# The feed-forward input projection as seven half-size products instead of eight (a two-layer decoder in one core)

## The chip, the cores and the metric

The kernel runs on one core of one Trainium2 chip. The metric is the device time of one execution in microseconds (us), the median of several runs.

## What is computed

Two decoder layers over 512 tokens of width 1024, all in float32. Each layer has a mixer of four branches, a cross-attention to 256 memory tokens, and a SwiGLU feed-forward part, each added to the residual stream `x`. The change touches the feed-forward part alone:

```python
def swiglu(h, w_in, w_out):
    a, b = jnp.split(h @ w_in, 2, axis=-1)
    return (jax.nn.silu(a) * b) @ w_out
...
x = x + swiglu(rmsnorm(x, norm_ffn_g[l]), w_ffn_in[l], w_ffn_out[l])
```

`w_in` is 1024 x 5632 (2 x 2816), `w_out` is 2816 x 1024.

## The kernel before

**Numbers in two pieces.** TensorE multiplies numbers of about 12 significant bits (type fp32r) at full rate. So every float32 operand is split into a rounded part `hi` and the rest `lo`, and a product is three matmuls: hi x hi, hi x lo, lo x hi (`mm3`, line 268). ScalarE makes `hi` by a copy, and VectorE or GpSimd makes `lo` by a subtraction with two inputs.

**The weight stream.** All weights lie in HBM in the order in which they are used, as blocks of 128 x 128, eight blocks (512 KB) to a chunk. `load` (line 227) has SyncE fetch a chunk. `prep` (line 240) makes its `hi` on ScalarE (line 245) and its `lo` (line 248) on GpSimd for three chunks out of five, on VectorE for the other two. `advance` prepares chunks up to three ahead of the one in use; there are four tiles for `hi` and four for `lo`, so the preparation of a chunk waits until TensorE has done with the chunk four before it.

**The order of work.** The program is written out as one Python run; each engine has one queue and works through it in that order. `fm` (line 274) makes products with features on the partitions: outputs are 128 columns of the weights by 512 tokens, one PSUM bank each, summed over the 128-row pieces k of the features. With `outer=True` four columns are summed side by side, so the first input piece serves four products before the second is needed. With `norm`, the statistics of the RMS norm are taken behind those products (`norm_stat`, line 384), the scale `rb` is broadcast by a matmul 18 matmuls later (`norm_bcast`, line 406), and only then are the four banks read out.

**The feed-forward part** (`ffn`, line 1093). Columns of `a` and `b` alternate, 44 in all, 8 pieces k each. `ev` reads an `a` bank (line 1101, times `rb`/2), takes its tanh on ScalarE (1102), forms (1 + tanh) x a (1106), reads the `b` bank (1108), multiplies (1109), and splits the result into `hi` and `lo` at once (lines 343 and 344). All 22 hidden pieces stay on chip in both parts. Then `w_ffn_out`: four output columns side by side over the 22 pieces, then the other four one after another. Each output column goes through `finish_x` (line 356): the bank is added to `x` on VectorE (361), ScalarE scales it (364) and VectorE makes the rest (365) for the next norm's input, ScalarE squares it (369, 372) and VectorE adds up the squares (376). In the last layer lines 364 and 365 are left out and ScalarE scales by the last gain (1132).

On chip there are 59 tiles of 128 x 512 (`unit`) and four tiles of 128 x 4 x 512 (`quad`).

Of the kernel before, what the change touches and what calls it, by code (L numbers as in the profile page):

```python
# [40 lines left out]
PREP = 3  # L41
LOAD = 5
# [15 lines left out]
class Prog:  # L58
    def __init__(self, tc, io):
# [3 lines left out]
        self.raw, self.wt = {}, {}  # L63
        self.nu, self.nq, self.vid = NU, NQ, 0
# [14 lines left out]
    def unit(self, n=1, r=False):  # L79
        """n tiles of [128, 512]; r: for products, of 12 significant bits"""  # L80
# [89 lines left out]
    def turn(self, key, n):  # L170
        """waits for the n-th turn at key"""
# [14 lines left out]
    def go(self, it):  # L186
        """one stage of an item; it yields how many beats its next stage should wait"""
# [39 lines left out]
    def load(self, n):  # L227
        while self.loaded < min(n, NCH):
            i = self.loaded
            r = self.wraw.tile([128, CHB * 128], F32, tag="raw", name="raw")  # L230
            self.nc.sync.dma_start(out=r, in_=self.io["wall"][i])
            self.raw[i] = r
            self.loaded += 1

    def advance(self, ci):
        while self.prepped < min(ci + PREP + 1, NCH):
            self.load(max(ci + LOAD, self.prepped) + 1)
            self.prep()

    def prep(self):  # L240
        nc = self.nc
        i = self.prepped
        r = self.raw.pop(i)
        h = self.whi.tile([128, CHB * 128], F32R, tag="hi", name="hi")
        nc.scalar.activation(out=h, in_=r, func=AF.Copy)  # L245
        lo = self.wlo.tile([128, CHB * 128], F32R, tag="lo", name="lo")
        eng = nc.gpsimd if i > 16 and i % 5 in self.pool_lo else nc.vector
        eng.tensor_tensor(out=lo, in0=r, in1=h.bitcast(F32), op=OP.subtract)  # L248
        self.wt[i] = (h, lo)
        self.prepped += 1  # L250

    def w(self, name, l, k, c0, n=1):
# [1198 lines left out]
```

## Time and profile before

| | before |
|---|---|
| time, median of 3 runs | 2343.83 us (2340.56 to 2344.4) |
| span of the profiled execution, first to last instruction | 2340.9 us |
| TensorE (PE) busy | 2285.5 us, 98% |
| weight loads (PEld) busy | 1835.9 us, 78% |
| VectorE (DVE) busy | 1170.2 us, 50% |
| ScalarE (ACT) busy | 820.9 us, 35% |
| GpSimd (POOL) busy | 656.2 us, 28% |
| mean granted TensorE clock | 0.993 of full speed |

The profile shows one execution. Its page gives the span and no other time of that execution; the span stands 2.9 us below the median of the runs. Busy times add up what the instructions of an engine took; matmuls overlap each other, so TensorE's pace is read from the starts of its matmuls, not from its busy share.

### The profile page before, as it was taken

What the parts mean: (1) busy time and instruction counts of PE and PEld (TensorE: products, weight loads), DVE (VectorE), ACT (ScalarE), POOL (GpSimd) and SP (SyncE); (2) the same over time, 40 slices, a digit from 0 to 9 for tenths busy, and PEclk for the clock granted to TensorE, in tenths of its full rate; (3) what the DMA queues carried; (4) which work ended last, traced back from release to release, by engine and by line L of the source; (5) the groups of instructions that cost most, each with busy time, mean ns of one, the idle gap of its engine ahead of it and who ended that gap; (6) DMA issues with size and microseconds to landing.
All of it is one profiled execution on the core that took longest, in us unless ns stands there. A gap on an engine that the chain in (4) does not pass through costs nothing. (4 is left out here: it accounts for less than half of the span.)

```text
span 2340.9 us, 27338 instructions
## 1 busy us (share of the span) xinstructions
PE 2285.5 (98%) x10714; PEld 1835.9 (78%) x10714; DVE 1170.2 (50%) x2186; ACT 820.9 (35%) x1395; POOL 656.2 (28%) x327
## 2 busy tenths in 40 slices
PE   8999999999999999999999999999999999999997
PEld 6777777777888788888877777777878877888886
DVE  6755443545846554431347563355475655543321
ACT  5323433343234432222323244334423443322231
POOL 2463222213222122222237422222322222222221
PEclk9999999999999999999999999999999999999998
DMA  6122222223234223333322222222223432332331
GB/s 227 51 81 73 78 76 73 81 72 95 78 99 144 72 90 108 99 92 107 122 88 80 67 79 73 73 81 76 92 68 99 138 105 81 90 99 90 100 98 54
DMA packets 61473, 213.70 MB, mean 91 GB/s; under 512 B 7072, under 2 KB 7456, under 8 KB 61088
## 3 DMA queue, kind: packets, MB, share of 16 engines
q1 hardware_dynamic: 60624, 210.18, 28.7%
q8 instruction: 84, 1.38, 0.2%
q10 hardware_dynamic: 576, 1.05, 0.1%
q0 software_dynamic: 144, 0.73, 0.1%
q14 instruction: 45, 0.37, 0.0%
HBM read 207.73 MB, written 4.19 MB: 91 GB/s over the span
## 5 line engine op out<-in xcount | busy, mean ns | idle before, releaser
L266 PE MATMUL ps<-u,hi 128*128 128x512 f32 x4160 | 1301.9, 394 | 1.3 <-ACT u L343 0.7
L248 POOL TENSOR_TENSOR lo<-raw,hi 128x1024 fp32r<-128x1024 f32 x213 | 519.0, 2438 | 1567.8 <-ACT hi L245 1505.3
L266 PEld LDWEIGHTS ps<-u,hi 128*128 128x128 f32 x4160 | 772.6, 188 | 173.8 <-issue 12.9
L266 PE MATMUL ps<-u,lo 128*128 128x512 f32 x2080 | 812.3, 391 | 1.7 <-POOL lo L248 1.7
L245 ACT ACTIVATE hi<-raw 128x1024 fp32r<-128x1024 f32 x372 | 388.8, 1051 | 329.9 <-PE ps L266 220.1
L266 PEld LDWEIGHTS ps<-u,lo 128*128 128x128 f32 x2080 | 391.0, 188 | 85.3 <-POOL lo L248 2.4
L248 DVE TENSOR_TENSOR lo<-raw,hi 128x1024 fp32r<-128x1024 f32 x159 | 209.5, 1320 | 352.2 <-ACT hi L245 351.9
L266 PE MATMUL ps<-hi,u 128*128 128x512 f32 x896 | 289.9, 405 | 11.6 <-ACT hi L245 11.6
L266 PE MATMUL ps<-q,hi 128*128 128x512 f32 x768 | 240.8, 395 | 0.0
L266 PEld LDWEIGHTS ps<-hi,u 128*128 128x128 f32 x896 | 166.1, 192 | 56.0 <-ACT hi L245 12.9
L266 PE MATMUL ps<-lo,u 128*128 128x512 f32 x448 | 178.2, 398 | 6.7 <-POOL lo L248 5.6
L266 PE MATMUL ps<-u 128*64 128x128 f32 (+6 forms) x1208 | 171.0, 338 | 4.3 <-DVE u L418 2.1
L266 PEld LDWEIGHTS ps<-q,hi 128*128 128x128 f32 x768 | 141.3, 188 | 34.0 <-issue 5.2
L266 PEld LDWEIGHTS ps<-u 128*128 128x128 f32 (+2 forms) x1208 | 117.1, 172 | 47.5 <-issue 27.9
L266 PE MATMUL ps<-q,lo 128*128 128x512 f32 x384 | 149.8, 390 | 0.0
L921 ACT ACTIVATE u<-u 128x512 f32<-128x512 f32 x64 | 40.4, 631 | 210.9 <-DVE u L920 210.6
L266 PEld LDWEIGHTS ps<-lo,u 128*128 128x128 f32 x448 | 85.7, 191 | 28.3 <-POOL lo L248 6.9
L920 DVE TENSOR_TENSOR u<-ps,u 128x512 f32<-128x512 f32 x64 | 44.0, 688 | 121.8 <-PE ps L266 121.8
L266 PEld LDWEIGHTS ps<-q,lo 128*128 128x128 f32 x384 | 72.1, 188 | 15.5
L1108 DVE TENSOR_TENSOR u<-ps,u 128x512 f32<-128x512 f32 x44 | 30.4, 692 | 86.7 <-PE ps L266 85.9
L347 PE MATMUL ps<-gcst,u 128*128 128x128 f32 x416 | 65.9, 274 | 5.9 <-DVE u L684 2.8
L347 PEld LDWEIGHTS ps<-gcst,u 128*128 128x128 f32 x416 | 51.2, 140 | 23.0 <-DVE u L684 4.1
(209 smaller groups left out, 1657.2 us busy)
## 6 DMA issues: line engine op xcount, KB each, us to landing
raw<-wall SPq DMA_DIRECT2D x372, 512.0 KB, 3.5
q<-memt SPq DMA_DIRECT2D x6, 512.0 KB, 6.4
q<-xt SPq DMA_DIRECT2D x2, 1024.0 KB, 7.6
u<-rot SPq DMA_DIRECT2D x8, 256.0 KB, 4.1
u<-xt SPq DMA_DIRECT2D x8, 256.0 KB, 6.0
xd<-u SPq DMA_DIRECT2D x8, 256.0 KB, 2.0
u<-xd SPq DMA_DIRECT2D x8, 256.0 KB, 5.0
out<-u SPq DMA_DIRECT2D x4, 256.0 KB, 2.7
```

Source lines behind the costliest of these rows:

```text
L245: nc.scalar.activation(out=h, in_=r, func=AF.Copy)
L248: eng.tensor_tensor(out=lo, in0=r, in1=h.bitcast(F32), op=OP.subtract)
L266: self.nc.tensor.matmul(out, lhsT=a, rhs=b, start=start, stop=stop)
L347: self.nc.tensor.transpose(out, src, self.ident)
L920: nc.vector.tensor_tensor(out=self.U(u), in0=ps, in1=self.U(self.rb), op=OP.mult)
L921: nc.scalar.activation(out=self.U(u), in_=self.U(u), func=AF.Tanh, scale=0.5)
L1108: nc.vector.tensor_tensor(out=self.U(t), in0=ps, in1=self.U(self.rb), op=OP.mult)
```

## The change

Of the 22 pairs of `a` and `b` columns the first three are made as before. For the other 19 the kernel takes one pair of weight columns (two column blocks) by the two halves of the features (4 pieces k each) by the two halves of the tokens (256 each) as a 2 x 2 product of blocks, and makes it by the scheme of Strassen and Winograd: seven block products of 4 k x 3 matmuls with 256 columns (84 in all) stand where 48 matmuls with 512 columns stood.

This needs sums on both sides. On the weight side a pair is two chunks in one `quad`; `prep_halves` makes it ready in four granules: part 0 takes two sums on VectorE (one instruction of 1024 elements per partition, one of 512) and a `lo` of 512, part 1 a third sum of 512 and a `lo` of 1024 on VectorE, parts 2 and 3 each a `lo` of 1024 on GpSimd. On the input side `operands` builds, once per layer and for each of four k, seven operands of 256 tokens from `x`: the norm is multiplied in (two instructions of 512), four sums, seven `hi` on ScalarE, four `lo` on VectorE and three on GpSimd. It is queued as stages behind the first four columns, and `finish("S")` has all of it in the queues before the first of the seven products.

On the output side ScalarE copies the bank of the first running sum out three times, and VectorE forms the four output quarters by four instructions of 256 columns out of PSUM; the gate then works on float32 tiles. The hidden pieces are no longer split when they are made: `split(k)` does it in the output projection, three pieces ahead of TensorE, once in each of three groups of output columns (4, 2, 2). `x` is overwritten by `operands`; it is written to HBM after the cross-attention and read back before the output projection.

```diff
-PREP = 3
-LOAD = 5
+FLY = 4
+RAWS = 3
+FF_PLAIN = 3
+OPS = ("A11", "A12", "A22", "S1", "S2", "S3", "S4")
...
+                q = self.quad()
+                for i in range(2):
+                    self.nc.sync.dma_start(out=self.Q(q)[:, 2 * i:2 * i + 2],
+                                           in_=self.io["wall"][c + i].rearrange("p (a b) -> p a b", a=2))
...
+    def advance(self, g):
+        while self.prepped < len(self.gran) and (self.prepped <= g or self.fly < FLY):
+            assert self.fly < FLY
+            self.load(4)
             self.prep()
+        self.load(4)
...
+    def prep_halves(self, c, part, h, lo):
+        nc, v = self.nc, self.nc.vector
+        B = self.Q(self.raw[c])
+        if part == 0:
+            self.sums = self.quad()
+        S = self.Q(self.sums) if part < 3 else None
+        n = 1 if part == 0 else 2
+        src = (B[:, 0:1], S[:, 0:2] if S is not None else None, S[:, 2:4] if S is not None else None, B[:, 2:4])[part]
+        h3, lo3 = (t.rearrange("p (a b) -> p a b", a=2)[:, :n] for t in (h, lo))
+        if part == 0:
+            v.tensor_tensor(out=S[:, 0:4:3], in0=B[:, 1:3], in1=B[:, 0:2], op=OP.subtract)
+            v.tensor_tensor(out=S[:, 1], in0=S[:, 3], in1=B[:, 0], op=OP.add)
+        nc.scalar.activation(out=h3, in_=src, func=AF.Copy)
+        if part == 1:
+            v.tensor_tensor(out=S[:, 2], in0=S[:, 1], in1=B[:, 3], op=OP.subtract)
+        eng = nc.gpsimd if part >= 2 else v
+        eng.tensor_tensor(out=lo3, in0=src, in1=h3.bitcast(F32), op=OP.subtract)
...
+    def operands(self, g):
+        nc, v = self.nc, self.nc.vector
+        H = T // 2
+        self.ops = []
+        for k in range(KD // 2):
+            a, b = self.x + k, self.x + k + KD // 2
+            for d in (k, k + KD // 2):
+                x = self.U(self.x + d)
+                v.scalar_tensor_tensor(out=x, in0=x, scalar=g[:, d:d + 1], in1=self.U(self.rb), op0=OP.mult, op1=OP.mult)
+            yield 1
+            A11, A21, A12, A22 = (self.U(u)[:, h * H:h * H + H] for u in (a, b) for h in range(2))
+            self.ops.append([self.unit(r=True) for _ in OPS])
+            s = self.unit(2)
+            S1, S2, S3, S4 = (self.U(u)[:, h * H:h * H + H] for u in (s, s + 1) for h in range(2))
+            v.tensor_tensor(out=S1, in0=A21, in1=A22, op=OP.add)
+            v.tensor_tensor(out=S2, in0=S1, in1=A11, op=OP.subtract)
+            v.tensor_tensor(out=S3, in0=A11, in1=A21, op=OP.subtract)
+            v.tensor_tensor(out=S4, in0=A12, in1=S2, op=OP.subtract)
+            yield 1
+            for i, src in enumerate((A11, A12, A22, S1, S2, S3, S4)):
+                u = self.ops[k][i]
+                hi = self.UR(u)[:, :H]
+                nc.scalar.activation(out=hi, in_=src, func=AF.Copy)
+                eng = nc.gpsimd if i in (0, 2, 5) else v
+                eng.tensor_tensor(out=self.UR(u)[:, H:], in0=src, in1=hi.bitcast(F32), op=OP.subtract)
...
+    def product(self, bank, op, w, o, first):
+        H = T // 2
+        i = OPS.index(op)
+        out = self.P(bank)[:, :H]
+        K = len(self.ops)
+        for k in range(K):
+            u = self.UR(self.ops[k][i])
+            s = slice((o * 4 + k) * 128, (o * 4 + k) * 128 + 128)
+            hi, lo = w[0][:, s], w[1][:, s]
+            mm = lambda a, b, start, stop: self.nc.tensor.matmul(out, lhsT=a, rhs=b, start=start, stop=stop,
+                                                                 skip_group_check=not first)
+            mm(hi, u[:, :H], first and k == 0, False)
+            mm(hi, u[:, H:], False, False)
+            mm(lo, u[:, :H], False, k == K - 1)
...
+            nc.scalar.activation(out=s1, in_=half(r1), func=AF.Copy)
+            self.advance(g[1])
+            r5 = self.bank()
+            self.product(r5, "S1", self.wt[g[1]], 0, True)
+            self.product(r1, "S2", self.wt[g[1]], 1, False)
+            nc.scalar.activation(out=s2, in_=half(r1), func=AF.Copy)
+            self.advance(g[2])
+            r3 = self.bank()
+            self.product(r3, "A22", self.wt[g[2]], 0, True)
+            self.product(r1, "S3", self.wt[g[2]], 1, False)
+            nc.scalar.activation(out=s3, in_=half(r1), func=AF.Copy)
+            self.advance(g[3])
+            v.tensor_tensor(out=o2[:, right], in0=half(r5), in1=s3, op=OP.add)
+            v.tensor_tensor(out=o1[:, right], in0=s3, in1=half(r3), op=OP.subtract)
+            r4 = self.bank()
+            self.product(r4, "A12", self.wt[g[3]], 1, True)
+            if j + 1 < len(pairs):
+                enter(j + 1)
+            v.tensor_tensor(out=o1[:, left], in0=half(r4), in1=s1, op=OP.add)
+            self.product(r5, "S4", self.wt[g[3]], 0, False)
+            v.tensor_tensor(out=o2[:, left], in0=half(r5), in1=s2, op=OP.add)
+            after(j)
...
+        def gate(a, b):
+            t = self.unit()
+            nc.scalar.activation(out=self.U(t), in_=self.U(a), func=AF.Tanh, scale=0.5)
+            nc.vector.scalar_tensor_tensor(out=self.U(a), in0=self.U(t), scalar=1.0, in1=self.U(a), op0=OP.add,
+                                           op1=OP.mult)
+            self.release(t)
+            nc.vector.tensor_tensor(out=self.U(a), in0=self.U(a), in1=self.U(b), op=OP.mult)
...
+        cols = [(j // 2) * 128 + (j % 2) * HID for j in range(2 * FF_PLAIN)]
+        self.fm("w_ffn_in", l, cols[:4], self.h(), ev, outer=True,
+                norm=lambda: self.add("S", self.operands(gf)))
         self.fm("w_ffn_in", l, cols[4:], self.h(), lambda j, ps: ev(j + 4, ps))
-        self.release(self.rbh)
+        self.finish("S")
...
+        self.load_x(self.xf)
...
+        def split(k):
+            hi, lo = self.unit(r=True), self.unit(r=True)
+            nc.scalar.activation(out=self.UR(hi), in_=self.U(hd[k]), func=AF.Copy, scale=0.5)
+            nc.vector.scalar_tensor_tensor(out=self.UR(lo), in0=self.U(hd[k]), scalar=0.5, in1=self.U(hi),
+                                           op0=OP.mult, op1=OP.subtract)
+            return hi, lo
+        d0, ready = 0, {}
+        groups = (4, 2, 2)
+        order = [(i, k) for i in range(len(groups)) for k in range(KH)]
+        ahead = iter(order)
+        def more(n):
+            while len(ready) < n and (nxt := next(ahead, None)):
+                ready[nxt] = split(nxt[1])
+        for i, n in enumerate(groups):
+            bs = [self.bank() for _ in range(n)]
+            for k in range(KH):
+                more(3)
+                hi, lo = ready[i, k]
+                for j in range(n):
+                    self.mm3(self.P(bs[j]), self.w("w_ffn_out", l, k, (d0 + j) * 128), (self.UR(hi), self.UR(lo)),
+                             k == 0, k == KH - 1)
+                del ready[i, k]
+                self.release(hi)
+                self.release(lo)
+                if i == len(groups) - 1:
+                    self.release(hd[k])
+            for j, b in enumerate(bs):
+                fin(d0 + j, self.P(b))
+            d0 += n
...
+        def fin(d, ps):
+            self.finish_x(d, ps, gf)
+            nc.sync.dma_start(out=self.xf[d], in_=self.U(self.x + d))
+        self.fm("w_xo", l, c4(0), os_, fin, outer=True, need=heads)
+        self.fm("w_xo", l, c4(512), os_, lambda j, ps: fin(4 + j, ps))
```

VectorE's queue behind the norm of layer 0's feed-forward part, before (lines as above):

```order
L1101 TENSOR_TENSOR u<-ps,u 128x512
L1106 SCALAR_TENSOR_TENSOR u<-u 128x512
L1108 TENSOR_TENSOR u<-ps,u 128x512
L1109 TENSOR_TENSOR u<-u 128x512
L344 TENSOR_TENSOR q<-u,q 128x512
```

And now: L1303 reads a bank, L1294 and L1297 are the gate, L1181 multiplies the norm into `x`, L1187 to L1190 are the four sums, L1197 the `lo` parts (this group of L1181 to L1197 stands there four times, all ahead of the first product):

```order
L1303 TENSOR_TENSOR u<-ps,u 128x512 x2
L1294 SCALAR_TENSOR_TENSOR u<-u 128x512
L1297 TENSOR_TENSOR u<-u 128x512
L1303 TENSOR_TENSOR u<-ps,u 128x512 x2
L1294 SCALAR_TENSOR_TENSOR u<-u 128x512
L1297 TENSOR_TENSOR u<-u 128x512
L1181 SCALAR_TENSOR_TENSOR u<-u,vec 128x512 x2
L1303 TENSOR_TENSOR u<-ps,u 128x512
L1187 TENSOR_TENSOR u<-u 128x256
L1188 TENSOR_TENSOR u<-u 128x256
L1189 TENSOR_TENSOR u<-u 128x256
L1190 TENSOR_TENSOR u<-u 128x256
L1197 TENSOR_TENSOR u<-u 128x256 x4
```

Where VectorE had only reads of banks, gates and splits, 40 instructions of the operands now stand between the gates and the first pair.

VectorE's queue for one pair of the 19, now. L311 and L312 (the two sums), L317 (`lo`, part 0), L315 (third sum) and L317 (`lo`, part 1) prepare the next pair's weights; L1268, L1269, L1275 and L1279 form the four quarters of this pair; L1294 and L1297 are its gate:

```order
L311 TENSOR_TENSOR q<-q 128x2x512
L312 TENSOR_TENSOR q<-q 128x512
L317 TENSOR_TENSOR lo<-q,hi 128x512
L315 TENSOR_TENSOR q<-q 128x512
L317 TENSOR_TENSOR lo<-q,hi 128x1024
L1268 TENSOR_TENSOR u<-ps,u 128x256
L1269 TENSOR_TENSOR u<-u,ps 128x256
L1275 TENSOR_TENSOR u<-ps,u 128x256
L1279 TENSOR_TENSOR u<-ps,u 128x256
L1294 SCALAR_TENSOR_TENSOR u<-u 128x512
L1297 TENSOR_TENSOR u<-u 128x512
```

Before, a pair had the five rows of the first fence and, for two chunks in five, one `lo` of 1024. The seventh product adds to the bank that L1268 reads, so it waits for L1268, and L1268 stands behind the weights of the next pair.

VectorE's queue in the output projection of layer 0, where the first four output columns are done, before:

```order
L361 TENSOR_TENSOR u<-ps,u 128x512
L365 SCALAR_TENSOR_TENSOR u<-u,vec 128x512
L376 TENSOR_TENSOR u<-u 128x512
L248 TENSOR_TENSOR lo<-raw,hi 128x1024 x2
L361 TENSOR_TENSOR u<-ps,u 128x512
```

And now (L439, L443 and L454 are what L361, L365 and L376 were; L1341 is the `lo` of a hidden piece, L293 that of a chunk):

```order
L439 TENSOR_TENSOR u<-ps,u 128x512
L443 SCALAR_TENSOR_TENSOR u<-u,vec 128x512
L454 TENSOR_TENSOR u<-u 128x512
L439 TENSOR_TENSOR u<-ps,u 128x512
L443 SCALAR_TENSOR_TENSOR u<-u,vec 128x512
L454 TENSOR_TENSOR u<-u 128x512
L1341 SCALAR_TENSOR_TENSOR u<-u 128x512
L293 TENSOR_TENSOR lo<-raw,hi 128x1024
L1341 SCALAR_TENSOR_TENSOR u<-u 128x512 x8
```

Ahead of the four `finish_x` stand 24 rows of L1341, for the 22 pieces of the first group and two of the second; the third piece of the second group stands behind them.

## Rows read from the trace of the kernel before

**Rows 1.** The page: the span, and each engine's busy time.

```profile
span 2340.9 us, 27338 instructions
...
PE 2285.5 (98%) x10714; PEld 1835.9 (78%) x10714; DVE 1170.2 (50%) x2186; ACT 820.9 (35%) x1395; POOL 656.2 (28%) x327
```

**Rows 2.** The chain that ended last, longest piece: start us, us, engine and line.

```profile
1988.10 334.39 PE ps L266 x1472
```

**Rows 3.** TensorE's timeline, plain columns, layer 0: start us, us, form, count.

```profile
1041.04 0.39 PE L266 MATMUL ps<-u,lo 128*128 128x512 f32 x1
...
1041.72 0.39 PE L266 MATMUL ps<-u,lo 128*128 128x512 f32 x1
```

**Rows 4.** TensorE's timeline: eight transposes of 128 columns in a run.

```profile
1656.16 1.04 PE L347 MATMUL ps<-gcst,u 128*128 128x128 f32 x8
```

**Rows 5.** Lines 248 and 1109: duration ns min/median/max.

```profile
L248 DVE TENSOR_TENSOR lo<-raw,hi x159: 1207/1225/3229, 9.4 to 2290.8; 128x1024 fp32r<-128x1024 f32 x159
...
L248 POOL TENSOR_TENSOR lo<-raw,hi x213: 2354/2397/2930, 100.3 to 2301.7; 128x1024 fp32r<-128x1024 f32 x107
...
L1109 DVE TENSOR_TENSOR u<-u x44: 691/692/2414, 853.8 to 2203.6; 128x512 f32<-128x512 f32 x44
```

**Rows 6.** Timeline of GpSimd and VectorE together, feed-forward input, layer 0.

```profile
875.34 5.22 POOL L248 TENSOR_TENSOR lo<-raw,hi 128x1024 fp32r<-128x1024 f32 x2 [4.90 <-ACT hi L245]
...
876.34 1.96 DVE L1106 SCALAR_TENSOR_TENSOR u<-u 128x512 f32<-128x512 f32 x1 [0.70 <-ACT u L1102]
...
879.13 1.98 DVE L1109 TENSOR_TENSOR u<-u 128x512 f32<-128x512 f32 x1
```

**Rows 7.** The same view where both engines work on 256 columns.

```profile
556.06 0.92 POOL L603 TENSOR_TENSOR u<-u 128x256 f32<-128x256 f32 x1
556.30 0.96 DVE L604 TENSOR_TENSOR u<-u 128x256 f32<-128x256 f32 x1
556.94 0.92 POOL L605 TENSOR_TENSOR u<-u 128x256 f32<-128x256 f32 x1
```

**Rows 8.** Groups of VectorE by form: busy us, mean ns; 256 columns out of PSUM.

```profile
L635 DVE TENSOR_TENSOR u<-ps,gcst 128x256 f32<-128x256 f32 x16 | 6.0, 415 | 2.9 <-PE ps L266 2.9
```

**Rows 9.** The page: ScalarE's `hi` of a chunk; DMA issues, KB, us to landing.

```profile
L245 ACT ACTIVATE hi<-raw 128x1024 fp32r<-128x1024 f32 x372 | 388.8, 1051 | 329.9 <-PE ps L266 220.1
...
u<-xd SPq DMA_DIRECT2D x8, 256.0 KB, 5.0
```

**Rows 10.** Timeline behind the first four columns of the feed-forward part, layer 0.

```profile
842.25 1.84 PE L266 MATMUL ps<-gcst,u 128*128 128x1 f32 x16
...
849.68 0.60 ACT L409 ACTIVATE u<-ps 128x512 f32<-128x512 f32 x1 [6.41 <-PE ps L266]
850.31 0.63 ACT L1123 ACTIVATE u<-u 128x512 f32<-128x512 f32 x1
```

**Rows 11.** Timeline, `finish_x` of four columns: first and last row, layers 0 and 1.

```profile
1121.03 0.69 DVE L361 TENSOR_TENSOR u<-ps,u 128x512 f32<-128x512 f32 x1 [12.14 <-PE ps L266]
...
1130.82 0.68 DVE L376 TENSOR_TENSOR u<-u 128x512 f32<-128x512 f32 x1
...
2260.63 1.37 DVE L361 TENSOR_TENSOR u<-ps,u 128x512 f32<-128x512 f32 x2 [6.70 <-PE ps L266]
...
2267.28 0.69 DVE L376 TENSOR_TENSOR u<-u 128x512 f32<-128x512 f32 x1 [0.70 <-ACT u L372]
```

**Rows 12.** TensorE's timeline: the first matmul after an idle stretch.

```profile
143.20 0.62 PE L266 MATMUL ps<-u,stri 128*128 128x512 f32 x1 [3.79 <-POOL u L795]
```

**Rows 13.** Busy time by stretch: us, five engines, PEclk, DMA share, GB/s.

```profile
143.43:146.84 3.41, 3.03 (x7) 2.15 (x7) 1.18 (x2) 0.60 (x1) 3.41 (x4) 0.50 0.00 0
```

**Rows 14.** Timeline of the last column's `finish_x`.

```profile
2322.51 0.69 DVE L361 TENSOR_TENSOR u<-ps,u 128x512 f32<-128x512 f32 x1 [12.88 <-PE ps L266]
2323.24 0.63 ACT L372 ACTIVATE u<-u 128x512 f32<-128x512 f32 x1 [13.57 <-DVE u L361]
```

More of the change, by code (lines that the diff above doesn't have):

```diff
@@ L224, in beat, with plan @@
             self.step()
-    def load(self, n):
[L228 to L237, printed above, removed]
+    def plan(self):
+        plain = lambda n: ["n"] * (n // CHB)
+        head = plain(64)
+        layer = lambda: plain(928 + 16 * FF_PLAIN) + ["s"] * FF_HALVES + plain(8 * KH)
+        kinds = head + layer() + layer()
+        gran, c = [], 0
+        for kind in kinds:
+            if kind == "n":
+                gran.append(("n", c, 0))
+                c += 1
+            else:
+                gran += [("s", c, i) for i in range(4)]
+                c += 2
+        assert c == NCH, (c, NCH)
+        return gran, {(c, i): n for n, (_, c, i) in enumerate(gran)}
@@ new lines, in load @@
+    def load(self, n):
+        for _ in range(n):
+            if self.loaded == len(self.gran):
+                return
+            kind, c, _ = self.gran[self.loaded]
+            if kind == "n":
+                if self.raws == RAWS:
+                    return
+                r = self.wraw.tile([128, CHB * 128], F32, tag="raw", name="raw")
+                self.nc.sync.dma_start(out=r, in_=self.io["wall"][c])
+                self.raw[c] = r
+                self.raws += 1
+                self.loaded += 1
+            else:
+                if self.pairs == 2:
+                    return
+                q = self.quad()
+                for i in range(2):
+                    self.nc.sync.dma_start(out=self.Q(q)[:, 2 * i:2 * i + 2],
+                                           in_=self.io["wall"][c + i].rearrange("p (a b) -> p a b", a=2))
+                self.raw[c] = q
+                self.pairs += 1
+                self.loaded += 4
@@ L246, in prep @@
         lo = self.wlo.tile([128, CHB * 128], F32R, tag="lo", name="lo")
[L247 to L250 removed]
+        if kind == "n":
+            r = self.raw.pop(c)
+            self.raws -= 1
+            nc.scalar.activation(out=h, in_=r, func=AF.Copy)
+            eng = nc.gpsimd if c > 16 and c % 5 in self.pool_lo else nc.vector
+            eng.tensor_tensor(out=lo, in0=r, in1=h.bitcast(F32), op=OP.subtract)
+        else:
+            self.prep_halves(c, part, h, lo)
@@ new lines, in prep @@
+        self.wt[self.prepped] = (h, lo)
+        self.prepped += 1
+        self.fly += 1
+    def prep_halves(self, c, part, h, lo):
[15 more added lines that the diff above has]
+        eng.tensor_tensor(out=lo3, in0=src, in1=h3.bitcast(F32), op=OP.subtract)
+        if part == 2:
+            self.release(self.sums, 4)
+        if part == 3:
+            self.release(self.raw.pop(c), 4)
+            self.pairs -= 1
@@ L252, in w, with done @@
+    def done(self, g):
+        if self.wt.pop(g, None):
+            self.fly -= 1
     def w(self, name, l, k, c0, n=1):
@@ L1120, in ffn @@
-        cols = [(j // 2) * 128 + (j % 2) * HID for j in range(2 * KH)]
-        def half():
-            self.rbh = self.unit()
-            nc.scalar.activation(out=self.U(self.rbh), in_=self.U(self.rb), func=AF.Copy, scale=0.5)
-        self.fm("w_ffn_in", l, cols[:4], self.h(), ev, outer=True, norm=half)
-        self.fm("w_ffn_in", l, cols[4:], self.h(), lambda j, ps: ev(j + 4, ps))
-        self.release(self.rbh)
+                ua[j] = u
+            else:
+                gate(ua.pop(j - 1), u)
```

118 lines of the change are left out of this document (76 added, 42 removed).

## The prediction

> **What bounds the kernel now.** I read the page first: TensorE is busy for 98% of the span, VectorE for 50%, ScalarE for 35%, GpSimd for 28% [rows 1]. The chain of waits says the same of the part that changes: from 1988 us to the end of layer 1's feed-forward part it is one piece of 334 us on TensorE [rows 2]. So there every matmul saved is time saved, as long as no other engine takes over. TensorE's timeline gives its pace: three matmuls of 512 columns from 1041.04 to 1041.72 [rows 3], 0.227 us each. A pair of `a` and `b` columns is 48 of them, 10.9 us.
>
> The averages hide who would take over. The timeline of GpSimd and VectorE does not [rows 6]. GpSimd starts a `lo` at 875.34; alone it takes 2.40 us [rows 5], so it is done at 877.74. VectorE starts a gate instruction with two inputs in SBUF at 876.34; it should take 0.69 us and ends at 878.30, 0.56 us after GpSimd. GpSimd's second `lo` is done at 875.34 + 5.22 = 880.56, which is 2.26 us after VectorE's end; VectorE's next one ends at 881.11, 0.55 us later. So the two take turns, with some 0.14 us of each hidden: in turns, 512 columns cost VectorE 0.55 us and 1024 columns cost GpSimd 2.26 us. On 256 columns the turns are 0.28 us (from 556.98 to 557.26) and 0.60 us (to 557.86) [rows 7]. The maxima of lines 248 and 1109, 3.2 and 2.4 us against 1.2 and 0.69 [rows 5], are such waits. With GpSimd rarely needed this cost nothing; the change needs both engines much more.
>
> **The products.** A pair becomes 84 matmuls of 256 columns, and no row shows one of this type. From below: each loads its own 128 x 128 weights, and eight transposes in a run, bound by such loads, take (1.04 - 0.27)/7 = 0.11 us each [rows 4], 0.27 being the last one's own duration. From above: 512 columns at 2.4 GHz are 0.213 us, so a matmul carries 0.0135 us beyond its columns; if that is paid whole for half the columns, 0.107 + 0.0135 = 0.120 us. If it shrinks with them it is half of 0.227, 0.1135; I take 0.114, nearest to that row. A pair is then 84 x 0.114 = 9.6 us of TensorE (9.2 to 10.1): 1.3 us less than now, 49 us for all 38 pairs, if nothing else binds.
>
> The Trainium skill (TensorE: Matmul & The Clock Gate, section Back-to-back issue gap) gives N/2.4 + 2.5 ns, an estimate of 0.109 us for 256 columns and 9.2 us for a pair. By it 512 columns would come every 0.216 us; the trace has 0.227, so it is too low here.
>
> **The pair as a loop.** The seventh product adds to a bank that VectorE must first read, and that read stands behind the next pair's weights in VectorE's queue (second place shown). From the end of one seventh product to the end of the next: bank out of TensorE 0.2; last quarter 0.41 [rows 8]; first gate instruction 0.69 and hand-over 0.03; then GpSimd's turn for part 3, 2.26, since ScalarE can make its `hi` only once the seventh product has freed the tile, 1.05 us earlier [rows 9]; second gate instruction 0.55; the sums of 1024 and 512 elements 1.17 and 0.72; `lo` of 512, 0.66; third sum 0.69; `lo` of 1024, 1.15 (1.22 less the overlap of neighbours) [rows 5]; the quarter that frees the bank 0.36; start of TensorE 0.1; seventh product 12 x 0.114 = 1.37. Sum 10.36; **10.4 us**, above TensorE's own 9.6, and only 0.5 below today's 10.9. GpSimd's other `lo` (part 2) falls beside the quarters, which read PSUM and are not held up. ScalarE, with four `hi` (0.6 + 3 x 1.05), three short copies and a tanh, is at some 5.5 us.
>
> Bounds: 9.6 if the turns cost nothing, 11.0 if each turn is a whole instruction and hand-overs add 0.3. For the 36 pairs that are not the first of a layer: 36 x (10.4 - 10.88) = **-17 us** (-46 to +4).
>
> The rows show turns that overlap by 0.14 us [rows 6]. The Trainium skill (SBUF — State Buffer, section Who interferes with whom) has the rule: a VectorE instruction with two SBUF inputs and a GpSimd instruction that reads SBUF exclude each other for the whole instruction. By that the loop is 10.7 us and the 36 pairs save 6 us; by the rows 17.
>
> **The operands.** The first product needs operands of all four k, and nothing is left for TensorE meanwhile. In layer 0, `rb` is copied out from 849.68 [rows 10]; TensorE then has 30 plain matmuls, to about 856.2. VectorE can start on the four banks at 850.2, since the half-scale copy [rows 10] is gone; four reads and two gates, 8 x 0.69, to 855.7. GpSimd's part 2 takes a turn, 2.26: 858.0. Then per k: two instructions of 512 at 0.69, four sums at 0.44, four `lo` at 0.36, 4.6 us, and of GpSimd's three `lo` some 1.4 us are not beside something else: 6.0. Two more columns and their gate lie between: 2.8. The first operand of the fourth k is there at 858.0 + 3 x 6.0 + 2.8 + 1.4 + 0.7 = 880.9, the one for the second product at 882.5. TensorE idles some 25 us. GpSimd then makes part 3 (its `hi` stood behind 28 operand copies), to 886.1, VectorE the next pair's weights and the quarter, 4.9 us, to 891.0, and the seventh product ends at 892.4. Today the pair would end at 856.2 + 10.9 = 867.1. **25.3 us** lost in a layer, 51 in both. Bounds: 19 without any turns (4.6 per k, no 2.26), 28 if every turn of GpSimd counts.
>
> **The output projection.** Its pieces are split as it goes. Behind the last seventh product stand quarter, two gate instructions and the first split: 0.2 + 0.41 + 0.72 + 0.69 + 0.69 less the one matmul that needs no `lo`, **2.5 us** a layer, 5 in both. Between groups TensorE holds two pieces ready, 2 x 6 x 0.227 = 2.7 us, while `finish_x` of the whole group stands ahead of the third (third place shown). Four of them take 1131.50 - 1121.03 = 10.5 us in layer 0 and 2267.97 - 2260.63 = 7.3 in layer 1 [rows 11]; with 0.2 before and 0.69 for the split, less 2.7, TensorE waits 8.7 and 5.5 us. Two of them, at half, leave 3.4 and 2.0. Together **20 us** (14 to 24). The clock: after 3.79 us of idling [rows 12] it stood at 0.50, 1.2 GHz, for the next 3.4 us [rows 13], a loss of 1.7. I count it behind the two longest waits here, **3 us** (0 to 10); behind the operands it is hidden, since VectorE is last there. At the end two `finish_x` instead of one stand before the norm: read 0.69, square 0.63 [rows 14] and sum 0.69 once more, **2 us**.
>
> **At no cost.** Storing and reloading `x`, 5.0 us to landing [rows 9]: the reload has the first group, 60 us, and weights behind it in SyncE's queue are six chunks ahead; uncovered it would cost those 5 us. Twice the splits: per piece 0.63 on ScalarE and 0.69 on VectorE against 1.36 us of matmuls; uncovered, a turn of GpSimd in front of some would add up to 1 us each.
>
> **Sum.** -17 + 51 + 5 + 20 + 3 + 2 = +64 us. The profiled span of 2341 becomes 2405; the median of the runs lies 3 us above the span, so **2408 us**.
>
> **Rivals.**
> *TensorE alone sets the pair (faster).* If a matmul of 256 costs only its columns, 0.107 us, and VectorE never holds the bank, a pair is 9.0 us: 36 x -1.9 = -68, with 38 for the operands without turns and 23 for the rest: -7, 2337 us. It is faster only below 9.1 us a pair. Against it: 0.227 instead of 0.213 [rows 3] and the turns [rows 6]. 5%. The page's 0.109 us, with the same 38 and 23, would end at 2344.
> *No turns, TensorE at 0.114.* Pair 9.6, operands 19: -46 + 38 + 30 = +22, 2366 us. For it: turns matter only where the engines meet, and GpSimd's part 3 might fall beside the quarters. 17%.
> *The loop is longer than today's pair.* Turns of whole instructions (10.7 us, +11 in all, if nothing else changes) and hand-overs among four engines, each small, bring it to 11.2 us and the operands to 28: 36 x 0.3 + 56 + 32 = +99, 2443 us. For it: every term of the loop is in series and each is at its best here; against it, the 0.14 us of overlap [rows 6]. 20%. The SBUF page's rule would be the first half of it.
> *The narrow matmul does not hide its load.* 0.11 + 0.107 = 0.218 us: a pair takes 18.3 us, 38 x 7.4 = +281 us. Against it: transposes of 128 columns come every 0.11 us, load included [rows 4]. 3%.
>
> **How the numbers follow.** The forecast has 55%. The range of 2362 to 2445 takes in it, the rivals at 2366 and 2443, and the bounds of the terms between. 0.2% of 2344 is 4.7 us, about what a measurement can tell from no change: to be faster needs the first rival, 5%; within 0.2% lies the best end of the second, 5%; slower is the rest, 90%.
>
> **What would show it.** Right: TensorE idle some 25 us ahead of the first pair in both layers, with VectorE busy on 256-column instructions; pairs every 10.4 us, TensorE waiting for VectorE before the seventh product, and instructions of both engines stretched where they meet; gaps of about 8.7 and 5.5 us between the first two groups of the output projection. Wrong: pairs at 9.6 us with no wait, or an idle stretch under 15 us; matmuls of 256 columns beyond 0.12 us would move the bound back to TensorE.

## The result and the profile after

The changed kernel takes 2430.32 us (median; 2424.4 to 2433.51), the kernel before beside it 2344.11 us: 1.036 times as long (95% interval 1.034 to 1.038). The profiled executions have spans of 2431.7 and 2340.9 us [rows 1], a difference of 90.8 us; the medians differ by 86.2, as the profiled execution after is the slowest of its four. The page of the kernel after, span and busy times:

```profile
span 2431.7 us, 31086 instructions
...
PE 2300.9 (95%) x12082; PEld 1901.9 (78%) x12082; DVE 1505.9 (62%) x2589; ACT 976.8 (40%) x1727; POOL 749.2 (31%) x382
```

TensorE is not busy for less time than before, but for 15 us more: where it waits, its clock falls, and its matmuls take longer there. To see where the 91 us lie, I cut both executions where TensorE's timeline shows the matmuls of one column that begin a norm. After:

```profile
854.59 1.84 PE L344 MATMUL ps<-gcst,u 128*128 128x1 f32 x16
...
1246.01 1.84 PE L344 MATMUL ps<-gcst,u 128*128 128x1 f32 x16
...
2036.88 1.84 PE L344 MATMUL ps<-gcst,u 128*128 128x1 f32 x16
...
2412.92 0.38 PE L344 MATMUL ps<-gcst,u 128*128 128x1 f32 x2 [1.55 <-DVE u L454]
```

Before, the first of the four stands at 842.25 [rows 10], the others are:

```profile
1204.47 1.84 PE L266 MATMUL ps<-gcst,u 128*128 128x1 f32 x16
...
1981.83 1.84 PE L266 MATMUL ps<-gcst,u 128*128 128x1 f32 x16
...
2322.31 0.28 PE L266 MATMUL ps<-gcst,u 128*128 128x1 f32 x2
```

Differences of the stages against the kernel before, in us, with the experiments that follow below:

| stage | after | e8 | e1 | e2 | e3 | e7 | e13 |
|---|---|---|---|---|---|---|---|
| mixer and attention, layer 0 | +12.3 | +9.2 | +2.1 | +12.1 | +13.1 | +5.0 | -0.8 |
| feed-forward, layer 0 | +29.2 | 0.0 | +27.3 | +15.7 | +22.6 | +3.7 | -3.0 |
| mixer and attention, layer 1 | +13.5 | +14.0 | +0.7 | +13.5 | +13.1 | 0.0 | +0.1 |
| feed-forward, layer 1 | +35.6 | 0.0 | +28.8 | +19.2 | +28.9 | +16.2 | -1.8 |
| tail | +0.2 | -0.4 | -1.2 | -1.2 | +0.2 | -1.2 | -0.7 |
| span | +90.8 | +22.8 | +57.6 | +59.3 | +78.0 | +23.7 | -6.2 |

The two feed-forward parts lose 65 us, what the prediction summed for them. The other 26 us lie in the mixers, whose arithmetic the change leaves alone.

**A pair.** Timeline of VectorE for one pair of layer 0, from one last quarter (L1279) to the next, and of its first pair (the bracket is the idle time ahead of an instruction, and who ended it):

```profile
903.25 0.42 DVE L1279 TENSOR_TENSOR u<-ps,u 128x256 f32<-128x256 f32 x1 [1.79 <-PE ps L1215]
...
954.43 0.42 DVE L1279 TENSOR_TENSOR u<-ps,u 128x256 f32<-128x256 f32 x1 [1.13 <-PE ps L1215]
954.77 0.68 DVE L1294 SCALAR_TENSOR_TENSOR u<-u 128x512 f32<-128x512 f32 x1
955.49 2.78 DVE L1297 TENSOR_TENSOR u<-u 128x512 f32<-128x512 f32 x1
958.19 1.21 DVE L311 TENSOR_TENSOR q<-q 128x1024 f32<-128x1024 f32 x1
...
961.31 1.23 DVE L317 TENSOR_TENSOR lo<-q,hi 128x1024 fp32r<-128x1024 f32 x1
962.45 0.42 DVE L1268 TENSOR_TENSOR u<-ps,u 128x256 f32<-128x256 f32 x1
...
964.66 0.43 DVE L1279 TENSOR_TENSOR u<-ps,u 128x256 f32<-128x256 f32 x1 [1.13 <-PE ps L1215]
```

The pair takes 964.66 - 954.43 = 10.23 us, and so do nearly all of the 36. The gate's second instruction (L1297) lasts 2.78 us instead of 0.69. GpSimd's timeline shows why, and behind it TensorE's shows its pace:

```profile
955.26 2.46 POOL L317 TENSOR_TENSOR lo<-q,hi 128x1024 fp32r<-128x1024 f32 x1 [0.51 <-ACT hi L313]
```

```profile
962.92 0.51 PE L1215 MATMUL ps<-u,hi 128*128 128x256 f32 x2
963.26 0.28 PE L1215 MATMUL ps<-u,lo 128*128 128x256 f32 x1
963.38 0.40 PE L1215 MATMUL ps<-u,hi 128*128 128x256 f32 x2
```

Matmuls of 256 columns follow each other every 0.120 us (963.26 to 963.38), so a pair is 84 x 0.120 = 10.08 us of TensorE. The seventh product (from 962.92) stands 0.15 us longer behind L1268. Loop and TensorE are all but tied.

**The operands.** TensorE's timeline behind the plain columns of layer 0, and a row of busy time by stretch (PE, PEld, DVE, ACT, POOL, then the granted clock):

```profile
871.00 0.58 PE L1215 MATMUL ps<-u,hi 128*128 128x256 f32 x1 [2.62 <-ACT u L1195]
...
883.71 0.58 PE L1215 MATMUL ps<-u,hi 128*128 128x256 f32 x1 [5.39 <-ACT u L1195]
```

```profile
870.70:894.60 23.90, 8.83 (x27) 6.44 (x28) 23.66 (x44) 12.67 (x32) 10.41 (x13) 0.50 0.00 0
```

These are two of four waits, one for each k (2.62, 4.12, 5.39 and 4.11 us). VectorE is busy for 23.7 of 23.9 us. TensorE's clock stands at 0.50 (1.2 GHz), with its short bursts between waits, and TensorE is idle for 17.4 of the 35.0 us from 868 to 903. VectorE is last for nearly all of this. At the end TensorE is: VectorE waits 1.79 us for its last bank at 903.25 and 1.13 us in the later pairs, so the half clock costs at most 0.7 us here (1.3 in layer 1). The last plain matmul starts at 867.99, the first pair ends at 903.25: 35.3 us, 24.4 more than a plain pair of 10.9.

**The output projection.** TensorE's waits in the first group and ahead of the second and third in layer 0, and at the last pair and in the first group in layer 1 (seven in all, from 1.8 to 5.9 us):

```profile
1088.93 0.50 PE L344 MATMUL ps<-u,hi 128*128 128x512 f32 x1 [1.78 <-DVE u L1341]
...
1159.03 0.79 PE L344 MATMUL ps<-u,hi 128*128 128x512 f32 x1 [5.88 <-ACT u L1340]
...
1194.75 0.49 PE L344 MATMUL ps<-u,hi 128*128 128x512 f32 x1 [2.59 <-ACT u L1340]
...
2270.87 0.80 PE L1215 MATMUL ps<-u,hi 128*128 128x256 f32 x2 [2.74 <-DVE u L1268]
2278.36 0.79 PE L344 MATMUL ps<-u,hi 128*128 128x512 f32 x1 [4.28 <-DVE u L1341]
```

L1340 and L1341 are the `hi` and `lo` of a hidden piece; between groups they stand behind the `finish_x` of the group that ends. In layer 0 the first `finish_x` of the first group starts 1.5 us before TensorE begins the second group, since the banks of the four columns are done one after another:

```profile
1148.81 0.68 DVE L439 TENSOR_TENSOR u<-ps,u 128x512 f32<-128x512 f32 x1
...
1150.27 0.62 PE L344 MATMUL ps<-u,hi 128*128 128x512 f32 x2
```

Behind each wait the clock falls, here at 1158.90 (columns as above):

```profile
1158.90:1164.30 5.40, 5.11 (x11) 3.75 (x12) 4.66 (x7) 3.10 (x6) 0.00 (x0) 0.50 0.30 97
```

**The mixers.** SyncE's DMA queue in layer 0's mixer. Before:

```profile
697.72 4.63 SPq L382 DMA_DIRECT2D u<-xt  x8
703.19 0.99 SPq L959 DMA_DIRECT2D q<-memt  x2
704.69 13.68 SPq L231 DMA_DIRECT2D raw<-wall  x4
```

After, the same loads behind three chunks of weights (L261):

```profile
694.01 15.79 SPq L261 DMA_DIRECT2D raw<-wall  x3
709.85 4.08 SPq L460 DMA_DIRECT2D u<-xt  x8
714.03 2.36 SPq L1037 DMA_DIRECT2D q<-memt  x2
```

What waits for them, from ScalarE's and TensorE's timelines together:

```profile
721.36 3.30 ACT L1054 ACTIVATE u<-q,vec 128x256 fp32r<-128x256 f32 x8 [7.98 <-DMA q<-memt]
...
725.65 0.79 PE L344 MATMUL ps<-u,hi 128*128 128x512 f32 x1 [4.55 <-ACT hi L291]
```

The memory tokens (`memt`) are asked for 11 us later. ScalarE waits 7.98 us for them (0.57 us before), the `hi` of a chunk behind that in its queue is late, and TensorE stands for 4.55 us. A like wait of 2.9 us is at 567.70, and three more are in layer 1 (4.05, 2.33 and 3.68 us; before, one of 1.73 us).

### The profile page after: what moved, and what is told of

Same layout as the page of the kernel before. It is cut to its first block, busy times and chain, and to the rows that moved or that the text cites. A ratio compares the mean times of both kernels' runs of the same rounds, so it can differ in the third digit from the quotient of the medians.

```text
span 2431.7 us, 31086 instructions
## 1 busy us (share of the span) xinstructions
PE 2300.9 (95%) x12082; PEld 1901.9 (78%) x12082; DVE 1505.9 (62%) x2589; ACT 976.8 (40%) x1727; POOL 749.2 (31%) x382
## 5 line engine op out<-in xcount | busy, mean ns | idle before, releaser
L344 PE MATMUL ps<-u,hi 128*128 128x512 f32 x3200 | 1022.3, 400 | 30.8 <-ACT u L1340 14.2
L293 POOL TENSOR_TENSOR lo<-raw,hi 128x1024 fp32r<-128x1024 f32 x168 | 409.9, 2441 | 1283.1 <-ACT hi L291 1235.6
L344 PEld LDWEIGHTS ps<-u,hi 128*128 128x128 f32 x3200 | 600.7, 191 | 174.1 <-ACT u L1340 16.1
L344 PE MATMUL ps<-u,lo 128*128 128x512 f32 x1600 | 632.1, 395 | 2.5 <-POOL lo L293 2.4
L1215 PE MATMUL ps<-u,hi 128*128 128x256 f32 x2128 | 398.8, 289 | 39.4 <-ACT u L1195 33.5
L1215 PEld LDWEIGHTS ps<-u,hi 128*128 128x128 f32 x2128 | 337.1, 194 | 48.7 <-ACT u L1195 36.1
L344 PEld LDWEIGHTS ps<-u,lo 128*128 128x128 f32 x1600 | 305.0, 191 | 70.2 <-POOL lo L293 3.3
L293 DVE TENSOR_TENSOR lo<-raw,hi 128x1024 fp32r<-128x1024 f32 x128 | 173.6, 1359 | 229.5 <-ACT hi L291 229.3
L1215 PE MATMUL ps<-u,lo 128*128 128x256 f32 x1064 | 303.9, 286 | 0.0
L344 PE MATMUL ps<-hi,u 128*128 128x512 f32 x896 | 290.3, 406 | 10.7 <-ACT hi L291 10.7
L317 POOL TENSOR_TENSOR lo<-q,hi 128x1024 fp32r<-128x1024 f32 x76 | 185.3, 2438 | 231.7 <-ACT hi L313 227.0
L344 PEld LDWEIGHTS ps<-hi,u 128*128 128x128 f32 x896 | 167.4, 193 | 55.0 <-ACT hi L291 11.6
L1215 PEld LDWEIGHTS ps<-u,lo 128*128 128x128 f32 x1064 | 207.2, 195 | 0.0
L313 ACT ACTIVATE hi<-q 128x1024 fp32r<-128x1024 f32 (+1 forms) x152 | 140.4, 946 | 105.9 <-DVE q L312 88.9
L1341 DVE SCALAR_TENSOR_TENSOR u<-u 128x512 fp32r<-128x512 f32 x132 | 126.6, 1012 | 57.3 <-ACT u L1340 57.3
```

The costliest lines, as they stand in the source:

```text
L313: nc.scalar.activation(out=h3, in_=src, func=AF.Copy)
L317: eng.tensor_tensor(out=lo3, in0=src, in1=h3.bitcast(F32), op=OP.subtract)
L344: self.nc.tensor.matmul(out, lhsT=a, rhs=b, start=start, stop=stop)
L1215: mm = lambda a, b, start, stop: self.nc.tensor.matmul(out, lhsT=a, rhs=b, start=start, stop=stop, skip_group_check=not first)
L1341: nc.vector.scalar_tensor_tensor(out=self.UR(lo), in0=self.U(hd[k]), scalar=0.5, in1=self.U(hi), op0=OP.mult, op1=OP.subtract)
```

## Experiments

**The weight queue.** `advance` now calls `load` once more after each preparation. Once all tiles are out, that load waits in SyncE's queue until a tile is free, with all that is behind it. e1 takes the call out:

```diff
             self.prep()
-        self.load(4)
```

> Edit: the changed kernel without the second call of load that follows each preparation, so that SyncE's queue holds no weight load whose tile is still in use ahead of the small loads of the mixers. Theory (the 23 us that the two mixers lost come from that queue): the mixers fall back to within 3 us of the kernel before, 2430 - 23 = about 2407 us, TensorE idle under 1 us at 557, 720, 1746, 1800 and 1902 us; the feed-forward parts stay as they are (pairs every 10.2 us). Rival A (the mixers lose to something else, such as the placing of tiles or the memory written and read back for x): unchanged, 2427 to 2433 us. Rival B (the load ahead is needed where the halved pairs use their weights): the mixers gain, but TensorE waits for weights in the pairs, and the time stays above 2415 us.

2406.58 us (2400.57 to 2409.53), 1.027 of before (1.025 to 1.029). As the theory has it: the mixers are within 2.1 and 0.7 us of before, and in SyncE's queue the same loads stand at 699.79 again:

```profile
691.28 8.45 SPq L261 DMA_DIRECT2D raw<-wall  x2
699.79 4.61 SPq L459 DMA_DIRECT2D u<-xt  x8
```

The feed-forward part of layer 1 gains too (35.6 to 28.8): the wait of 4.28 us at the output projection is 1.8 us, with less of the half clock behind it. e8 puts such a load into the kernel before:

```diff
             self.load(max(ci + LOAD, self.prepped) + 1)
             self.prep()
+            self.load(self.prepped + LOAD - PREP + 1)
```

> Edit: the kernel before with one more weight chunk asked for after each preparation, and nothing else; it has no Strassen scheme in it. Theory (a load that waits in SyncE's queue for its tile holds up the small loads behind it): the mixers lose as they did in the changed kernel, 2344 + 10 to 25 = 2354 to 2369 us, with TensorE idle near 557 and 720 us in layer 0, and the feed-forward parts unchanged. Rival (the mixers' loss belongs to the scheme): 2340 to 2348 us.

2365.68 us (2365.48 to 2370.52), 23 us above the kernel before, 1.010 (1.009 to 1.012). The same loss in the same place, without a single product of the scheme, and the same row in SyncE's queue:

```profile
691.72 15.80 SPq L231 DMA_DIRECT2D raw<-wall  x3
```

The rival that the loss belongs to the scheme falls. A load more "ahead" was a load more in front of others.

**What sets the pair.** Three runs leave out a third of the products' matmuls, so that TensorE has room (one execution each: 2426, 2338 and 2389 us):

```diff
             mm(hi, u[:, :H], first and k == 0, False)
-            mm(hi, u[:, H:], False, False)
-            mm(lo, u[:, :H], False, k == K - 1)
+            mm(hi, u[:, H:], False, k == K - 1)
```

> Edit: the seven products leave out their lo x hi matmuls, so that a pair has 56 narrow matmuls instead of 84 and TensorE's own work falls from 10.08 to 6.72 us (56 x 0.120); every other engine does the same work. Theory (a loop through VectorE and a turn of GpSimd stands just behind TensorE): the loop loses only the four matmuls of the seventh product that lie in it, 10.23 - 4 x 0.120 = 9.75; a pair comes every 9.6 to 9.9 us, with TensorE idle some 3 us in each ahead of the seventh product. Rival (TensorE alone sets the pair and the other engines have room): 6.7 to 7.2 us a pair.

The pairs come every 10.33 us in layer 0 and 10.28 in layer 1 (means without each layer's last; 9.7 to 11.3), as slowly as with all the matmuls. That TensorE alone sets the pair is out. But the theory's 9.6 to 9.9 is missed too: every other pair meets its 9.75, and only for a while. The timeline of GpSimd and VectorE shows what the four shorter matmuls ran into:

```profile
960.95 2.40 POOL L317 TENSOR_TENSOR lo<-q,hi 128x1024 fp32r<-128x1024 f32 x1 [4.86 <-ACT hi L313]
...
962.91 0.99 DVE L1293 SCALAR_TENSOR_TENSOR u<-u 128x512 f32<-128x512 f32 x1
963.93 2.95 POOL L317 TENSOR_TENSOR lo<-q,hi 128x1024 fp32r<-128x1024 f32 x1 [0.58 <-POOL lo L317]
963.93 0.69 DVE L1296 TENSOR_TENSOR u<-u 128x512 f32<-128x512 f32 x1
...
964.54 3.42 DVE L311 TENSOR_TENSOR q<-q 128x1024 f32<-128x1024 f32 x1
```

The gate starts earlier and meets GpSimd's part 2, which it just missed before (0.99 instead of 0.68 us); part 3 then takes its turn ahead of L311, 3.42 instead of 1.21 us.

Next, GpSimd out of the pairs altogether, on top of that edit:

```diff
-        eng = nc.gpsimd if part >= 2 else v
-        eng.tensor_tensor(out=lo3, in0=src, in1=h3.bitcast(F32), op=OP.subtract)
+        if part >= 2:
+            nc.scalar.activation(out=lo3, in_=src, func=AF.Copy)
+        else:
+            v.tensor_tensor(out=lo3, in0=src, in1=h3.bitcast(F32), op=OP.subtract)
```

> Edit: as in the kernel with two matmuls of three, and in addition the lo of weight parts 2 and 3 is not formed: ScalarE writes a copy in its place, so that GpSimd does nothing in the pairs. ScalarE then has about 5.5 + 2 x 1.05 = 7.6 us a pair. Theory (GpSimd's part 3 takes a turn of 2.26 us ahead of the second gate instruction, and each engine holds the other out): the loop falls by the turn, and the gate instruction behind it gets its 0.14 us back: 9.75 - 2.26 + 0.14 = 7.6; a pair every 7.5 to 7.9 us. Rival (the two engines do not hold each other out, and L1297 is late for another reason): 9.6 to 9.9 us as with GpSimd.

Every pair but a layer's last takes 7.67 us, and L1298 (L1297 above) is back at 0.69 us:

```profile
955.88 0.42 DVE L1280 TENSOR_TENSOR u<-ps,u 128x256 f32<-128x256 f32 x1 [0.64 <-PE ps L1217]
...
956.94 0.69 DVE L1298 TENSOR_TENSOR u<-u 128x512 f32<-128x512 f32 x1
...
963.54 0.42 DVE L1280 TENSOR_TENSOR u<-ps,u 128x256 f32<-128x256 f32 x1 [0.64 <-PE ps L1217]
```

And part 3 on VectorE, which so gets 1.2 us of work more (again with two matmuls of three):

```diff
-        eng = nc.gpsimd if part >= 2 else v
+        eng = nc.gpsimd if part == 2 else v
```

> Edit: as in the kernel with two matmuls of three, and in addition VectorE makes the lo of weight part 3 itself, behind the second gate instruction, where GpSimd made it before; GpSimd keeps part 2. VectorE then has more work of its own. Theory (it is GpSimd's turn that the loop pays, 2.26 us, and 1.15 us on VectorE are cheaper): 9.75 - 2.26 + 0.14 + 1.15 = 8.8; a pair every 8.6 to 9.0 us although VectorE is given more to do. Rival (VectorE's own work sets the loop, turns or not): 9.75 + 1.15 = 10.9 us a pair.

9.2 us in the mean (8.80 to 9.98), a little above what the theory gives and far under its rival's 10.9. More work on VectorE made the loop shorter by 1.1 us. Why only a part of the pairs reach 8.8 stays open.

**More cover for the operands.** Six plain pairs instead of three:

```diff
-FF_PLAIN = 3
+FF_PLAIN = 6
```

> Edit: the changed kernel with six plain pairs instead of three ahead of 16 halved ones, so that TensorE has 33 us more of plain work while the operands are built. Theory (the operands' 25 us a layer are latency that TensorE had nothing to cover with): both stalls go, less three pairs a layer at 10.9 instead of 10.23: 2430 - 50 + 6 x 0.65 = about 2385 us, with TensorE idle under 2 us ahead of the first halved pair. Rival (VectorE and GpSimd are full there, and the gates of the added plain pairs take the time that the operands need): a stall of over 10 us a layer remains, 2405 to 2434 us.

2397.02 us (2394.11 to 2401.96), 1.023 (1.021 to 1.026): between the two. Busy time by stretch (columns as above) shows what is left:

```profile
900.00:905.00 5.00, 3.18 (x20) 2.58 (x18) 4.93 (x9) 1.69 (x2) 0.00 (x0) 1.00 0.00 2
905.00:910.00 5.00, 2.04 (x12) 1.84 (x13) 4.80 (x7) 3.42 (x5) 3.10 (x2) 0.83 0.00 0
```

The added pairs cover most of the stall (the feed-forward parts gain 13.5 and 16.4 us), but VectorE is full to the end, 4.9 of 5 us, and some 5 us of idling remain in a layer.

**The finish in the next group** (`fin` of a finished group's columns called one at a time):

```diff
                 more(3)
+                if pend and k % 3 == 1:
+                    flush()
                 hi, lo = ready[i, k]
```

> Edit: the changed kernel with the finish of each output column of the output projection put into the next group (one column at every third hidden piece) and the first split put ahead of the last quarter of the last pair. Theory (the gaps between groups are the finish standing in VectorE's queue ahead of the next group's splits): the gaps of 6.3, 3.0, 4.0 and 2.4 us go and the half clock behind them too (20 us at 0.50, some 10 us of loss); the last group's finish stays. 2430 - 15.6 - 5 to 10 = about 2405 to 2410 us. Rival (VectorE is short of time in the output projection, so the splits are late wherever the finish stands): the same idle time comes back inside the groups, over 2420 us.

2420.57 us (2418.67 to 2422.15), 1.033 (1.031 to 1.035): 10 us of the 20 to 25 that the theory gives, so the rival has most of it. The gaps between groups go, but one `finish_x` (3 x 0.69), three splits and a share of the weights' `lo` are more than the 4.1 us that TensorE takes for three pieces of two columns, and waits of up to 1.98 us come back inside the group, ended by the `lo` of a split.

**Repairs together.** e7 is e1, eight plain pairs, and the finish at every fifth piece:

```diff
-FF_PLAIN = 3
+FF_PLAIN = 8
...
-        self.load(4)
...
+                if pend and k % 5 == 1:
+                    flush()
```

> Edit: three repairs together on the changed kernel: no load ahead after a preparation; eight plain pairs instead of three ahead of 14 halved ones; the finish of an output column put into the next group (one at every fifth hidden piece) and the first split ahead of the last quarter. Theory (the three losses are separate and add): 2430 - 24 for the queue, - 33 as with six plain pairs and - 20 for what was still idle there, + 3 for two pairs fewer a layer, - 16 for the finish: about 2340 us, 2333 to 2350. Then 14 pairs x 2 x 0.65 = 18 us of gain stand against what is still lost at the boundaries. Rival (the losses share one cause, VectorE's load, and come back elsewhere): over 2360 us.

2370.2 us (2366.7 to 2370.34), 1.010 (1.009 to 1.012): 30 us short of the sum. The mixers are repaired (the 5 us left in layer 0 arise in its first 220 us; their cause stays open), but layer 1's feed-forward part still loses 16 us. TensorE's longest wait there, from the table of waits:

```profile
PE ps L343 <- DVE lo L292: 6.4, 1, 6.4
```

The operands in VectorE's queue now made the `lo` of a plain chunk late. e11 spreads their stages out and takes part 3 from GpSimd; e12 is the same with six plain pairs and `yield 2`:

```diff
-FF_PLAIN = 8
+FF_PLAIN = 7
...
-            yield 1
+            yield 3
...
-        eng = nc.gpsimd if part >= 2 else v
+        eng = nc.gpsimd if part == 2 else v
...
-                more(3)
+                more(4)
```

> Edit on the kernel with the three repairs (2368 us): seven plain pairs instead of eight, the stages of the operands spread over the whole stretch of plain columns (one stage every third step instead of every step), the lo of weight part 3 on VectorE, splits four pieces ahead instead of three. Theory: the wait of 6.6 us in layer 1, where the operands in VectorE's queue made the lo of a plain chunk late, goes with the half clock behind it (- 8); with part 3 on VectorE the loop through VectorE falls under TensorE's own work and pairs come every 84 x 0.120 = 10.08 us instead of 10.23 (30 pairs, - 4.5); shorter waits inside the output projection (- 4); one plain pair fewer a layer (- 1): about 2350 us, 2343 to 2357. Rival (VectorE's load, not the place of its work, sets these stretches): over 2362 us, pairs still at 10.2.

2352.72 us (2347.24 to 2359.79), 1.004 (1.0025 to 1.0053), in the theory's range. The pairs come every 10.08 us, which is TensorE's own 84 x 0.120; what each of the other edits is worth was not measured apart:

```profile
953.07 0.42 DVE L1280 TENSOR_TENSOR u<-ps,u 128x256 f32<-128x256 f32 x1 [1.93 <-PE ps L1214]
963.15 0.42 DVE L1280 TENSOR_TENSOR u<-ps,u 128x256 f32<-128x256 f32 x1 [1.92 <-PE ps L1214]
```

> Edit: as in the run with paced operands, but six plain pairs, with a stage of the operands every second step. Theory (with pacing, six plain pairs, 72 us of TensorE with the first columns, are enough to hide the operands): 1.3 to 1.6 us faster than with seven. Rival (VectorE is full in that stretch, 4.9 of 5 us in the run with six plain pairs and no pacing): a stall of some 5 us a layer stays, 5 to 12 us slower than with seven.

2353.74 us (2349.14 to 2358.26), 1.0045 (1.003 to 1.006): neither; six and seven can't be told apart.

Last, on e12, no `lo` on GpSimd in the output projection:

```diff
-            eng = nc.gpsimd if c > 16 and c % 5 in self.pool_lo else nc.vector
+            eng = nc.gpsimd if c > 16 and c % 5 in self.pool_lo and c not in self.outc else nc.vector
```

> Edit on the run with six plain pairs and paced operands (2354 us): in the output projection VectorE makes the lo of every weight chunk, so that GpSimd does nothing there. VectorE gets 13 more lo of 1.22 us a layer. Theory (the waits of 1.5 to 2.3 us inside the output projection, 17 us a layer pair with the half clock behind them counted, are splits that stand through a turn of GpSimd, 2.45 us instead of 0.69): the waits at 1141, 1148, 2288 and 2307 us go, 5 to 10 us faster, 2343 to 2349: level with the kernel before. Rival (VectorE is full there, so the work taken from GpSimd costs as much as the turns): 2351 us or more.

2341.24 us (2336.46 to 2343.11), 0.9988 (0.9979 to 0.9997). The splits (group of their line: busy us, mean ns) fall from this in e12

```profile
L1320 DVE SCALAR_TENSOR_TENSOR u<-u 128x512 fp32r<-128x512 f32 x132 | 129.1, 1027 | 49.2 <-ACT u L1319 49.2
```

to this in e13:

```profile
L1323 DVE SCALAR_TENSOR_TENSOR u<-u 128x512 fp32r<-128x512 f32 x132 | 87.7, 715 | 4.6 <-ACT u L1322 4.6
```

VectorE took on the work of GpSimd (27 `lo` more) and got 41 us back that it had spent standing: all its busy time falls from 1453.4 us to 1436.5. So the best version that I found is level with the kernel before, 0.1% under it. Its 32 pairs save 32 x 0.8 = 26 us; the feed-forward parts are only 5 us shorter.

## Why the prediction was right, and where it was not

The forecast of 2408 us was 22 us short, inside its range; slower was right. Its steps, in us for both layers:

| step | predicted | measured |
|---|---|---|
| matmul of 256 columns | 0.114 (0.11 to 0.120) | 0.120 |
| loop of a pair | 10.4 | 10.23 |
| 36 pairs | -17 | -23 |
| operands | 51 | 50 (24.4 and 25.5) |
| boundary to the output projection | 5 | 9 (1.8; 2.7 + 4.3) |
| gaps between groups | 20 | 14 (5.9 + 2.6 + 3.6 + 2.0) |
| clock | 3 | 13 |
| tail (last plain matmul to the end: 18.8, then 20.7) | 2 | 2 |
| **sum, feed-forward parts and tail** | **64** | **65** |
| mixers, under "at no cost" | 0 | 26 |

- **The step that failed** is the part "At no cost". It weighed the reload of `x` and the weights in SyncE's queue, but not the second `load` of `advance`, which the diff shows: it changes the order of that queue in the whole program, ahead of every small load of the mixers. e1 takes 24 us out with it, e8 brings in 23 us alone.
- **Matmul.** What a matmul carries beyond its columns (0.0135 us) is paid whole for half the columns: 0.107 + 0.0135 = 0.120, the upper bound. I had taken the row nearest in form; the better reading of [rows 3] was a fixed part. The Trainium skill (TensorE: Matmul & The Clock Gate, section Back-to-back issue gap) gives 0.109 by its N/2.4 + 2.5 ns, which it calls the gap of an isolated matmul; the trace of this stream has 0.120.
- **Loop.** Mechanism and size held: each engine stands through the other's turn, and the pair ends 0.13 us under the sum. That TensorE would have 0.8 us of slack failed with the matmul; it has 0.15. e4 and e5 show that the turns hold the pair at 10.3 even when TensorE needs only 6.7, and that without GpSimd it is then 7.67. By the rule of the Trainium skill (SBUF — State Buffer, section Who interferes with whom) of whole instructions the loop was 10.7; L1297 ends 0.55 us after GpSimd, so 0.14 us of its 0.69 lie beside GpSimd's instruction, as in [rows 6], and the pair is 10.23.
- **Operands.** The size is right within 1 us, the chain through VectorE only in its first part, so this is in part luck. The first operand of the fourth k is there 21 us behind the plain columns (25 predicted), and from there the pair takes 14 us (11.5 predicted), at its end by TensorE's own work and not by the wait for GpSimd's part 3 and VectorE. TensorE idles for 17 and 19 us, not 25, and in four waits of at most 5.8 us, because the first product uses each k as it comes. e2 shows that it is not latency alone: with 33 us more of cover VectorE is full and 5 us a layer stay.
- **Clock.** Mis-sized. I counted it behind the two longest waits. The trace shows 0.50 behind all seven waits around the output projections, and the 5.9 us wait brings 6.8 us of it. The matmuls of 512 columns that started 0.32 to 0.68 us apart there instead of 0.227 add up to 11.6 us, the narrow ones of the last pairs to 1.1: 13 us.
- **Group gaps.** Too large by 6: I let `finish_x` begin 0.2 us behind the group's end, where it begins 1.5 us ahead of it, and I waited for the `lo` of the third piece, where TensorE starts with its `hi`, 0.9 us earlier. The boundary was too small by 4: in layer 1 the next chunk's `lo` (2.39 us, a turn) stood ahead of the last pair's L1268, and the gate stood through another turn.

Of the rivals, "TensorE alone sets the pair" falls with e4, "no turns" with e5, and the narrow matmul hides its load (0.120 us, not 0.218). The rival at 2443 us lies nearer to the measured time than the forecast does, but the pair of 11.2 us that it rests on did not come. That the feed-forward sum came out within 1 us owes something to terms that erred in opposite ways.

## What to carry to other kernels

A product saved on TensorE is worth only what the other engines leave of it: here 0.65 us a pair of the 1.36 that seven products for eight promise, against sums and splits that have to run beside other work, with cover for their start. A line that asks for data earlier is a change to a queue: list everything that comes behind it there, in the whole program and not only in the part that is changed. And where VectorE and GpSimd hold each other out, taking work from GpSimd can relieve VectorE even when VectorE gets all of it.

## What was not expected of the hardware

A matmul of 256 columns comes every 0.120 us, 53% of the 0.227 us of one with 512, so halving the columns costs 6% of the rate. TensorE's clock fell to 0.50 behind waits as short as 1.8 us, for some 3.4 us; I had counted on it only behind the longest. And a third of the matmuls left out of the pairs (28 of 84) changed their pace by nothing: 10.23 us with them, 10.28 to 10.33 without.
